# The inverse root of the row norms: from VectorE to GpSimd

## The chip, the cores and the metric

The kernel runs on one core of a Trainium2 chip as a single launch. The core has five engines with a queue each: TensorE (PE in the profile, with its weight loads apart as PEld), VectorE (DVE), ScalarE (ACT), GpSimd (POOL) and SyncE (SP, which here only issues DMAs). Each engine takes its instructions in a fixed order; an instruction that waits holds up everything behind it on its engine. The metric is the device time of one launch in microseconds (us), less is better.

## The reference

Two networks run one after the other on 256 tokens of width 1024. The first has two layers, each with a gated delta rule branch and a sliding window attention; the second has two layers, each of a gated feed-forward part, a mixer with two kinds of attention, and a second feed-forward part, on a latent stream and a context stream of 256 tokens each. What matters here is that every part ends by a norm over the 1024 columns of its output, a residual sum, and another norm over the sum that feeds the next part:

```python
def rmsnorm(x, g):
    xf = x.astype(jnp.float32)
    y = xf * lax.rsqrt(jnp.mean(xf * xf, axis=-1, keepdims=True) + EPS)
    return (y * g.astype(jnp.float32)).astype(x.dtype)
...
    mix = (jax.nn.sigmoid(gate_a) * y_a + jax.nn.sigmoid(gate_b) * y_b) @ w_o
    x = x + rmsnorm(mix, post_mix_g)

    h2 = rmsnorm(x, pre_mlp_g)
    ff = jnp.square(jax.nn.relu(h2 @ w_ff1)) @ w_ff2
    return x + rmsnorm(ff, post_mlp_g)
```

## The kernel before

All matrix products are made from weights that stream in from memory: `wtile` (L239) loads a raw tile by DMA, ScalarE makes its high part `hi` (L210) and VectorE the rest `lo` (L198), and TensorE adds three products for each tile (`mm3`, L264 to L266). Between these, VectorE also accumulates a product with the conditioning vector (`acc<-araw,csil,acc`, L201), which is needed later and has low priority.

A stream has 256 tokens, worked as two blocks of 128 (`tb` 0 and 1). `out_proj` (L1067) ends a part. For each block it makes two PSUM tiles of 512 columns. ScalarE squares both and sums the rows (`junk<-mm`, into the two columns of `ss`), and VectorE multiplies by the gain (`d`, or `acc` where partial sums were kept). Then, at a raised priority (`high_priority`, L1092), `inv_root` (L413) turns the two sums into 1/sqrt of their sum: `ms` is the sum, `rs` the integer guess, `rq_h` minus half of `ms`, and three Newton steps write `rq_t` and `rs` in turn. That is nine VectorE instructions on a single column of 128 rows, eight of them in a chain. The result scales `d` into the residual stream `xh` (or `xc`, the context; L201, two halves). At once the next norm of the same block begins (`nx.run`): `row_rs` (L420) squares the two halves of the new `xh` on ScalarE, calls `inv_root` again, and the row is scaled by the second root (`xn`, half by VectorE at L205, half by ScalarE at L210). The transposes of `xn` (TensorE, L405 in the first network and L1148 in the second) start the next part.

So each block of each part needs two inverse roots one behind the other, from the last product of the part to the first transposes of the next. The transposes are put off by `DEFER`: TensorE has products of the other block, and of the next weights, in between. A scheduler of the program's build sets the order of each engine's instructions, by priority and by when it takes an operand to be ready; a change of one engine's instructions can so reorder the others.

GpSimd makes four constants at the start and clears the tile `qz` twelve times (L1289) for the attentions of the second network; it has nothing else to do. The build calls `inv_root` 58 times: twice at the start, 28 times in `out_proj`, and for 28 rows that feed a next part. The other use of `rsqrt` (several columns at a time) isn't touched.

Of the kernel before, what the change touches and what calls it, by code (L numbers as in the profile page):

```python
# [11 lines left out]
I32 = mybir.dt.int32  # L12
AF = mybir.ActivationFunctionType
ALU = mybir.AluOpType
# [3 lines left out]
P = 128  # L18
# [16 lines left out]
MAGIC = 1597463007.0  # L35
# [128 lines left out]
class Kern:  # L164
# [38 lines left out]
    def ts(self, out, a, s1, op0, s2=None, op1=None):  # L203
        if op1 is None:
            self.nc.vector.tensor_scalar(out, a, s1, None, op0=op0)  # L205
        else:
            self.nc.vector.tensor_scalar(out, a, s1, s2, op0=op0, op1=op1)
# [203 lines left out]
        self.act(junk[:, :a.shape[-1]], a, AF.Square, scale=scale, accum_out=out)  # L411

    def inv_root(self, ss, eps):  # L413
        v = self.t(self.small, [P, 1], "ms", bufs=4)
        self.ts(v, ss[:, 0:1], ss[:, 1:2], ALU.add, eps, ALU.add)
        rs = self.t(self.small, [P, 1], "rs", bufs=4)
        self.rsqrt(rs, v, 1)
        return rs

    def row_rs(self, st, tb):  # L420

# [1086 lines left out]
```

## Time and profile before

| what | value |
|---|---|
| median of 3 runs (lowest, highest) | 2869.26 us (2864.54, 2869.78) |
| the profiled execution's own time | 2872.72 us |
| its span in the profile | 2870.9 us |
| granted clock of TensorE over the span | 0.989 |
| TensorE busy | 2790.4 us, 97% |
| VectorE busy | 2130.9 us, 74% |
| ScalarE busy | 1334.1 us, 46% |
| GpSimd busy | 5.2 us in 16 instructions |

The span runs from the first to the last instruction that the profile shows; 1.8 us of the profiled time lie outside it. Busy shares are means over the whole span, and TensorE's ends of instructions are modelled. Where TensorE waits is read from its idle time and from what ended it.

### The profile page before, as it was taken

How to read it: one execution, taken by the hardware profiler on the slowest of the kernel's cores; microseconds unless marked ns; L12 is line 12 of the kernel's file. 1: busy time of each engine (PE TensorE's matmuls, PEld its weight loads, DVE VectorE, ACT ScalarE, POOL GpSimd, SP SyncE). 2: the span in 40 equal slices, each digit the busy share in tenths (PEclk: the TensorE clock that was granted, in tenths of full speed). 3: DMA queues.
4: the chain of work that ended last, by engine and by line, in shares of the span. 5: the costliest groups of instructions: out<-in, count | busy, mean ns of one | idle time of the engine just before them, and what ended most of it. 6: DMA issues, size and time to landing. Idle time of an engine off the chain costs nothing.

```text
span 2870.9 us, 51232 instructions
## 1 busy us (share of the span) xinstructions
PE 2790.4 (97%) x19840; PEld 2594.7 (90%) x19840; DVE 2130.9 (74%) x5043; ACT 1334.1 (46%) x2627; POOL 5.2 (0%) x16
## 2 busy tenths in 40 slices
PE   8999999999999999999999999999999999999998
PEld 7999988889999888999988988998989989888897
DVE  7888668898886788878699788877686554766664
ACT  6555454565554655332243656332353323546553
POOL 0000000000000000000000000000000000000000
PEclk9999999999999999999999999999999999999999
DMA  6542457655325576455435242555444543341564
GB/s 220 171 118 72 142 178 236 201 181 159 92 74 177 175 222 198 136 159 160 134 114 167 77 138 82 165 151 162 138 131 141 150 125 96 98 131 44 153 197 140
DMA packets 443908, 416.76 MB, mean 145 GB/s; under 512 B 18320, under 2 KB 383760, under 8 KB 443664
## 3 DMA queue, kind: packets, MB, share of 16 engines
q1 hardware_dynamic: 443664, 413.49, 47.4%
q8 instruction: 156, 2.56, 0.4%
q14 instruction: 88, 0.72, 0.1%
HBM read 412.37 MB, written 1.05 MB: 144 GB/s over the span
## 4 chain that ended last, share of the span: by engine, by line
PE 81%; DVE 10%; ACT 4%; DMA 4%; issue 2%; SPq 0%; DVEq 0%; ACTq 0%
PE mm L264 22%; PE mm L265 22%; PE mm L266 22%; DVE lo L198 2%; PE sm L563 2%; PE sm L515 2%; ACT hi L210 2%; DMA araw<-in_w_ada 1%; PE sm L552 1%; PE sm L805 1%; DVE acc L201 1%; PE sm L800 1%; PE sm L264 1%; PE sm L265 1%; PE sm L266 1%
## 5 line engine op out<-in xcount | busy, mean ns | idle before, releaser
L198 DVE TENSOR_TENSOR lo<-raw,hi 128x1024 fp32r<-128x1024 f32 (+2 forms) x628 | 750.9, 1207 | 323.2 <-ACT hi L210 321.8
L210 ACT ACTIVATE hi<-raw 128x1024 fp32r<-128x1024 f32 (+2 forms) x628 | 647.9, 1047 | 717.4 <-PE mm L265 295.7
L264 PE MATMUL mm<-xTh,hi 128*128 128x256 f32 x2336 | 650.9, 279 | 3.0 <-ACT xTh L210 3.0
L265 PE MATMUL mm<-xTh,hi 128*128 128x256 f32 x2336 | 651.5, 279 | 0.8 <-DVE xTh L201 0.8
L266 PE MATMUL mm<-xTh,lo 128*128 128x256 f32 x2336 | 650.4, 279 | 0.0
L264 PEld LDWEIGHTS mm<-xTh,hi 128*128 128x128 f32 x2336 | 440.7, 189 | 3.7 <-ACT xTh L210 3.5
L265 PEld LDWEIGHTS mm<-xTh,hi 128*128 128x128 f32 x2336 | 441.3, 189 | 1.5 <-DVE xTh L201 1.2
L266 PEld LDWEIGHTS mm<-xTh,lo 128*128 128x128 f32 x2336 | 441.0, 189 | 0.1
L201 DVE SCALAR_TENSOR_TENSOR acc<-araw,csil,acc 128x256 f32<-128x256 f32 x896 | 391.3, 480 | 64.4 <-DMA araw<-in_w_ada 61.7
L264 PE MATMUL mm<-hi,hid 128*128 128x512 f32 x872 | 341.2, 391 | 0.0
L266 PE MATMUL mm<-hi,hid 128*128 128x512 f32 x872 | 340.3, 390 | 0.0
L265 PE MATMUL mm<-lo,hid 128*128 128x512 f32 x872 | 340.2, 390 | 0.0
L264 PE MATMUL mm<-xTc,hi 128*128 128x256 f32 x1104 | 306.2, 277 | 0.0
L265 PE MATMUL mm<-xTc,hi 128*128 128x256 f32 x1104 | 305.9, 277 | 0.0
L266 PE MATMUL mm<-xTc,lo 128*128 128x256 f32 x1104 | 305.6, 277 | 0.0
L265 PEld LDWEIGHTS mm<-xTc,hi 128*128 128x128 f32 x1104 | 207.3, 188 | 0.4
L264 PEld LDWEIGHTS mm<-xTc,hi 128*128 128x128 f32 x1104 | 207.3, 188 | 0.4
L266 PEld LDWEIGHTS mm<-xTc,lo 128*128 128x128 f32 x1104 | 207.3, 188 | 0.1
L266 PEld LDWEIGHTS mm<-hi,hid 128*128 128x128 f32 x872 | 164.0, 188 | 34.3
L265 PEld LDWEIGHTS mm<-lo,hid 128*128 128x128 f32 x872 | 164.2, 188 | 33.7 <-DVE lo L198 0.3
L264 PEld LDWEIGHTS mm<-hi,hid 128*128 128x128 f32 x872 | 164.1, 188 | 33.2
L264 PE MATMUL mm<-hi,xTh 128*128 128x256 f32 (+3 forms) x512 | 180.1, 353 | 4.9 <-ACT xTh L1157 3.4
(323 smaller groups left out, 4665.0 us busy)
## 6 DMA issues: line engine op xcount, KB each, us to landing
raw<-in_ffn_wi SPq DMA_DIRECT2D x352, 256.0 KB, 3.6
araw<-in_w_ada SPq DMA_DIRECT2D x288, 256.0 KB, 2.9
raw<-in_w_ff SPq DMA_DIRECT2D x128, 512.0 KB, 4.2
raw<-in_w_in SPq DMA_DIRECT2D x116, 512.0 KB, 3.9
raw<-in_ffn_wo SPq DMA_DIRECT2D x88, 512.0 KB, 4.1
raw<-in_w_o SPq DMA_DIRECT2D x40, 512.0 KB, 3.4
raw<-in_w_in SPq DMA_DIRECT2D x24, 432.0 KB, 4.8
raw<-in_w_up_sw SPq DMA_DIRECT2D x16, 512.0 KB, 3.8
```

The source lines that it names most:

```text
L198: self.nc.vector.tensor_tensor(out=out, in0=a, in1=b, op=op)
L201: self.nc.vector.scalar_tensor_tensor(out=out, in0=a, scalar=s, in1=b, op0=op0, op1=op1)
L210: self.nc.scalar.activation(out, a, func, **kw)
L264: mm(ps, lhsT=ah, rhs=bh, start=first, stop=False)
L265: mm(ps, lhsT=ah, rhs=bl, start=False, stop=False)
L266: mm(ps, lhsT=al, rhs=bh, start=False, stop=last)
L515: nc.tensor.matmul(ps[:, h, o:o + n], lhsT=q, rhs=k, start=m == 0, stop=m == len(qk) - 1)
L552: nc.tensor.transpose(ps[:, b, :], sc[:, b // nb, (b % nb) * P:(b % nb + 1) * P], self.ident)
L563: nc.tensor.matmul(po[:, h, :], lhsT=pT[:, h * nb + kb, :], rhs=v, start=kb == 0, stop=kb == nb - 1)
L800: nc.tensor.matmul(ps[:, i, :], lhsT=LT[:, i, :], rhs=Dm[:, i, :], start=True, stop=True)
L805: nc.tensor.matmul(ps[:, i, :], lhsT=DT[:, i, :], rhs=M[:, i, :], start=True, stop=True)
```

## The change

`inv_root` no longer calls `rsqrt`. It issues the same nine steps as GpSimd instructions on the same kind of columns; `t*(-0.5 v)` and `(t+1.5)*y` become one two-operation instruction each, with columns as scalars.

```diff
     def inv_root(self, ss, eps):
-        v = self.t(self.small, [P, 1], "ms", bufs=4)
-        self.ts(v, ss[:, 0:1], ss[:, 1:2], ALU.add, eps, ALU.add)
-        rs = self.t(self.small, [P, 1], "rs", bufs=4)
-        self.rsqrt(rs, v, 1)
-        return rs
+        v, y, nh, t = (self.t(self.small, [P, 1], x, bufs=4) for x in ("ms", "rs", "rq_h1", "rq_t1"))
+        ts = self.nc.gpsimd.tensor_scalar
+        ts(v, ss[:, 0:1], ss[:, 1:2], eps, op0=ALU.add, op1=ALU.add)
+        ts(y.bitcast(I32), v.bitcast(I32), -0.5, MAGIC, op0=ALU.mult, op1=ALU.add)
+        ts(nh, v, -0.5, None, op0=ALU.mult)
+        for _ in range(3):
+            ts(t, y, y, nh, op0=ALU.mult, op1=ALU.mult)
+            ts(y, t, 1.5, y, op0=ALU.add, op1=ALU.mult)
+        return y
```

The build also gives other orders. At the start of GpSimd's queue stood the constants, and behind them the first clearing of `qz`. Now there stand, behind the constants, an instruction without operands (its line is that of the first step) and the nine steps of the first root (`ms_103` from the sums `ss_98`; `rs_104` is the root):

```order
L1508 UNCONDITIONAL_BRANCH
L416 ISA
L416 TENSOR_SCALAR ms_103<-ss_98 128x1
L417 TENSOR_SCALAR rs_104<-ms_103 128x1
L418 TENSOR_SCALAR rq_h_16_105<-ms_103 128x1
L420 TENSOR_SCALAR rq_t_17_106<-rs_104,rq_h_16_105 128x1
L421 TENSOR_SCALAR rs_104<-rq_t_17_106,rs_104 128x1
L420 TENSOR_SCALAR rq_t_17_106<-rs_104,rq_h_16_105 128x1
L421 TENSOR_SCALAR rs_104<-rq_t_17_106,rs_104 128x1
L420 TENSOR_SCALAR rq_t_17_106<-rs_104,rq_h_16_105 128x1
L421 TENSOR_SCALAR rs_104<-rq_t_17_106,rs_104 128x1
```

All 58 roots stand there in this form, 522 instructions; the clearings of `qz` come between them.

On VectorE, at the end of the first layer's mixer (block 0, the row `xn_4356` of `xh_78`), this stood before between the multiplication by the gain `gpre` and the scaling by the second root `rs_4364`:

```order
L198 TENSOR_TENSOR xn_4356<-xh_78,gpre_364 128x1024
L207 TENSOR_SCALAR ms_4362<-ss_4357 128x1
L198 TENSOR_TENSOR lo_4497<-raw_4502,hi_4496 128x1024
L207 TENSOR_SCALAR rs_4364<-ms_4362 128x1
L205 TENSOR_SCALAR rq_h_738_4366<-ms_4362 128x1
L198 TENSOR_TENSOR d_4406<-mm_4379,gbc_4238 128x512
L201 SCALAR_TENSOR_TENSOR rq_t_737_4365<-rs_4364,rq_h_738_4366 128x1
L198 TENSOR_TENSOR lo_4507<-raw_4508,hi_4506 128x1024
L201 SCALAR_TENSOR_TENSOR rs_4364<-rq_t_737_4365,rs_4364 128x1
L198 TENSOR_TENSOR lo_4517<-raw_4518,hi_4516 128x1024
...
L205 TENSOR_SCALAR xn_4356<-xn_4356,rs_4364 128x512
```

The same place after the change, from the same multiplication on (the root is now `rs_4363`):

```order
L198 TENSOR_TENSOR xn_4356<-xh_78,gpre_364 128x1024
L198 TENSOR_TENSOR lo_4497<-raw_4498,hi_4496 128x1024
L205 TENSOR_SCALAR xn_4356<-xn_4356,rs_4363 128x512
L198 TENSOR_TENSOR lo_4497<-raw_4502,hi_4496 128x1024
L198 TENSOR_TENSOR d_4406<-mm_4379,gbc_4238 128x512
L198 TENSOR_TENSOR lo_4507<-raw_4508,hi_4506 128x1024
L198 TENSOR_TENSOR lo_4517<-raw_4518,hi_4516 128x1024
```

The scaling moved ahead of three weight splits and one multiplication by the gain; it stands behind one split only, and holds up those behind it until GpSimd's root is there.

On TensorE, at the end of a feed-forward part of the second network (context block 0, `xn_16747`), the transposes stood before behind eight products of the tile `mm_16910`, which belongs to a later block:

```order
L266 MATMUL mm_16810<-hi_2535_16644,hid_16523 128x512
L264 MATMUL mm_16910<-hi_16614,hid_15587 128x512
L265 MATMUL mm_16910<-lo_16615,hid_15587 128x512
...
L265 MATMUL mm_16910<-lo_16615,hid_15880 128x512
L1148 MATMUL sm_16839<-cst_76,xn_16747 128x128 x4
L1148 MATMUL sm_16851<-cst_76,xn_16747 128x128 x4
```

Now they stand in front of them (L1152 is the same line of the changed file):

```order
L266 MATMUL mm_16810<-hi_2535_16644,hid_16523 128x512
L1152 MATMUL sm_16839<-cst_76,xn_16747 128x128 x4
L1152 MATMUL sm_16851<-cst_76,xn_16747 128x128 x4
L264 MATMUL mm_16910<-hi_16614,hid_15587 128x512
L265 MATMUL mm_16910<-lo_16615,hid_15587 128x512
```

The transposes moved ahead of eight products. The transposes stand ahead of work that they stood behind at eleven more of the 26 places where a block's norm lies between two parts, by one to some fifty products each; at most of the others they stand where they stood.

## Rows read from the trace of the kernel before

**Rows 1.** The page's first part: busy us, share of the span, instructions.
```profile
PE 2790.4 (97%) x19840; PEld 2594.7 (90%) x19840; DVE 2130.9 (74%) x5043; ACT 1334.1 (46%) x2627; POOL 5.2 (0%) x16
```

**Rows 2.** Waits of PE by what ended them: us in total, times, longest us.
```profile
PE sm L405 <- DVE xn L205: 20.8, 5, 10.7
...
PE sm L1148 <- DVE xn L205: 8.7, 6, 2.5
```

**Rows 3.** Timeline of DVE, then PE, first layer's mixer end: start us, us, what [idle].
```profile
368.62 0.21 DVE L207 TENSOR_SCALAR ms<-ss 128x1 f32<-128x1 f32 x1 [4.50 <-ACT junk L210]
...
370.74 0.16 DVE L201 SCALAR_TENSOR_TENSOR rs<-rq_t,rs 128x1 f32<-128x1 f32 x1
...
374.54 0.21 DVE L207 TENSOR_SCALAR ms<-ss 128x1 f32<-128x1 f32 x1
374.67 1.22 DVE L198 TENSOR_TENSOR lo<-raw,hi 128x1024 fp32r<-128x1024 f32 x1
...
380.19 0.16 DVE L201 SCALAR_TENSOR_TENSOR rs<-rq_t,rs 128x1 f32<-128x1 f32 x1
...
378.07 0.39 PE L265 MATMUL mm<-lo,mT 128*128 128x512 f32 x1
378.29 0.39 PE L266 MATMUL mm<-hi,mT 128*128 128x512 f32 x1
380.93 1.18 PE L405 MATMUL sm<-cst,xn 128*128 128x128 f32 x8 [2.25 <-DVE xn L205]
```

**Rows 4.** Timeline of DVE, then PE, at context block 0 of the second network.
```profile
1472.44 0.21 DVE L207 TENSOR_SCALAR ms<-ss 128x1 f32<-128x1 f32 x1
...
1475.92 0.16 DVE L201 SCALAR_TENSOR_TENSOR rs<-rq_t,rs 128x1 f32<-128x1 f32 x1
...
1478.47 0.21 DVE L207 TENSOR_SCALAR ms<-ss 128x1 f32<-128x1 f32 x1
...
1482.34 0.15 DVE L201 SCALAR_TENSOR_TENSOR rs<-rq_t,rs 128x1 f32<-128x1 f32 x1
...
1483.64 1.07 PE L1148 MATMUL sm<-cst,xn 128*128 128x128 f32 x8 [2.52 <-DVE xn L205]
```

**Rows 5.** Stretches behind two such waits: busy (count) PE, PEld, DVE, ACT, POOL, clock.
```profile
382.00:385.50 3.50, 3.34 (x16) 3.23 (x16) 3.40 (x10) 0.74 (x2) 0.00 (x0) 0.51 0.69 209
385.50:389.00 3.50, 3.50 (x31) 3.50 (x31) 3.41 (x7) 2.98 (x7) 0.00 (x0) 1.00 0.73 253
...
586.90:590.30 3.40, 2.82 (x9) 2.08 (x8) 3.40 (x9) 0.00 (x0) 0.00 (x0) 0.50 0.26 92
590.30:593.70 3.40, 3.40 (x11) 3.14 (x10) 1.17 (x6) 1.18 (x2) 0.00 (x0) 0.50 0.54 153
593.70:597.00 3.30, 3.30 (x18) 3.15 (x17) 2.77 (x6) 2.08 (x4) 0.00 (x0) 1.00 0.40 94
```

**Rows 6.** Timeline of PE: the three other transposes that waited over 2.2 us.
```profile
569.50 1.67 PE L405 MATMUL sm<-cst,xn 128*128 128x128 f32 x8 [2.97 <-DVE xn L205]
...
585.13 1.07 PE L405 MATMUL sm<-cst,xn 128*128 128x128 f32 x8 [2.52 <-DVE xn L205]
...
944.24 1.16 PE L405 MATMUL sm<-cst,xn 128*128 128x128 f32 x8 [2.28 <-DVE xn L205]
```

**Rows 7.** Instructions on the tiles rs and ms: ns min/median/max, first to last.
```profile
L207 DVE TENSOR_SCALAR ms<-ss x58: 162/210/216, 7.5 to 2863.7; 128x1 f32<-128x1 f32 x58
L207 DVE TENSOR_SCALAR rs<-ms x58: 142/148/155, 7.8 to 2864.4; 128x1 int32<-128x1 int32 x58
L205 DVE TENSOR_SCALAR rq_h<-ms x58: 141/145/150, 7.8 to 2864.4; 128x1 f32<-128x1 f32 x58
...
L201 DVE SCALAR_TENSOR_TENSOR rq_t<-rs,rq_h x174: 177/217/223, 8.0 to 2865.5; 128x1 f32<-128x1 f32 x174
L201 DVE SCALAR_TENSOR_TENSOR rs<-rq_t,rs x174: 122/158/163, 8.3 to 2865.8; 128x1 f32<-128x1 f32 x174
```

**Rows 8.** Timeline of DVE: first and last of the 58 roots.
```profile
7.51 0.21 DVE L207 TENSOR_SCALAR ms<-ss 128x1 f32<-128x1 f32 x1
...
9.16 0.16 DVE L201 SCALAR_TENSOR_TENSOR rs<-rq_t,rs 128x1 f32<-128x1 f32 x1
...
2863.65 0.21 DVE L207 TENSOR_SCALAR ms<-ss 128x1 f32<-128x1 f32 x1 [4.75 <-ACT junk L210]
...
2865.77 0.16 DVE L201 SCALAR_TENSOR_TENSOR rs<-rq_t,rs 128x1 f32<-128x1 f32 x1
```

**Rows 9.** Timeline of POOL.
```profile
0.34 0.11 POOL L1500 MEMSET const-uint8-127<- 128x1 uint8 x1
1505.68 2.75 POOL L1289 MEMSET qz<- 64x384 f32 x6 [1505.23 <-PE mm L266]
```

## The prediction

> **What bounds the kernel now.** I read the busy times first. TensorE is busy for 2790.4 us, 97% of a span of 2870.9 us, and GpSimd for 5.2 us [rows 1]. So the 1.6 us or so of VectorE work per root are worth nothing as work: only places where TensorE stands still can be won or lost. I therefore read the waits of TensorE next, by what ended them. Two rows belong to this change: transposes of a normed row `xn` that wait for VectorE's scaling of it, 20.8 us in 5 waits in the first network and 8.7 us in 6 in the second [rows 2]. One of the eleven, of 10.7 us, is the start of the kernel. The other ten make 20.8 + 8.7 - 10.7 = 18.8 us; five of them are longer than 2.2 us.
>
> Third, the two timelines around such a wait. At the end of the first layer's mixer the first root runs from 368.62 to 370.90, the second from 374.54 to 380.35, with a 1.22 us weight split `lo` in the middle of it; TensorE's other products end at 378.68, and the transposes start at 380.93 after 2.25 us of idleness [rows 3]. The two chains are 2.28 + 5.81 = 8.09 us. At context block 0 of the second network they are 3.64 + 4.02 = 7.66 us, and the wait is 2.52 us [rows 4].
>
> Fourth, the stretch behind a wait. For 3.5 us after the transposes of that first place the granted clock is 0.51, the lower level (1.2 GHz), and TensorE gets through 16 products; in the next 3.5 us the clock is 1.00 and it does 31 [rows 5]. That wait so costs another 1.7 us. The five waits over 2.2 us are this one, that of context block 0 and three more of 2.97, 2.52 and 2.28 us [rows 6]. I read such a stretch behind each, and behind the one at 585 us it is twice as long, 586.9 to 593.7 at a clock of 0.50 [rows 5]: six times 1.7 = 10.2 us. In all, what a better or worse root can move at these places is 18.8 + 10.2 = 29 us, 1% of the time, and a good deal more if it gets worse.
>
> **The change, part by part.** *Nine instructions leave VectorE, 58 times.* By the medians one root is 0.210 + 0.148 + 0.145 + 3 x (0.217 + 0.158) = 1.63 us of busy time [rows 7], 94 us in all, out of an engine that is busy for 74% [rows 1]. From start to end a chain with nothing between its steps takes 1.81 us (7.51 to 9.32), one with one multiplication between 2.28 us (2863.65 to 2865.93) [rows 8]; with splits between, 3.6 to 5.8 us [rows 3, 4]. What leaves is therefore not 1.8 us of a path but often twice that, because other work of VectorE sits inside the chain.
>
> *Nine instructions come to GpSimd.* Nothing can sit inside them there but a clearing of `qz`. No row shows a GpSimd instruction that reads anything. Two rows bound one step. A clearing of one column takes 0.11 us, and six clearings of 64x384 take 2.75 us, 0.46 each [rows 9]. VectorE's step is 1.81 / 9 = 0.20. A dependent step has to read, compute and write one column: more than the first row, with far fewer elements than the second. I take 0.30, the middle, above VectorE's own step; this is an estimate. With 0.2 us for the hand-over from ScalarE and to VectorE (an estimate, about one VectorE step) a root takes L = 9 x 0.30 + 0.2 = 2.9 us. Its ends are 9 x 0.11 + 0.2 = 1.2 and 9 x 0.46 + 0.2 = 4.3 us.
>
> *What this does at a place.* New wait = old wait + 2L - old pair + the work that the transposes were moved ahead of. At the mixer's end nothing moved: 2.25 + 5.80 - 8.09 is below 0, the wait is gone, and the slow stretch with it. At context block 0 the transposes now stand ahead of eight products of 0.22 us from start to start (378.07 to 378.29 in [rows 3]), 1.8 us: 2.52 + 5.80 - 7.66 + 1.8 = 2.5, no gain at all. I made the same sum at all 26 places, with the spare time of those that do not wait now. The waits add up to 0.5 us for L = 1.8, 1.3 for 2.0, 5.6 for 2.5, 11.2 for 2.9, 13 for 3.0, 27 for 3.5, 46 for 4.0 and 58 for 4.3; waits over 2 us are none up to 2.5, two at 2.9, five at 3.5, about fifteen at 4.3. The sum is steep, because the order has spent the slack: where transposes moved forward, nothing covers a longer root.
>
> *The ends.* At the start and the end nothing covers a root. The first goes from 1.81 to 2.9 (+1.1), the last from 2.28 to 2.9 (+0.6), and the second block of the start is late by about as much as the first (+1): +2.7 us.
>
> *VectorE's order.* The scaling by the root now stands behind one `lo` and in front of three and a `d`, and holds them up until GpSimd is done. VectorE is busy for 3.40 of 3.50 us just there [rows 5], so this cover is not free: per block it no longer does 2 x 1.63 = 3.3 us of steps, and stands at the scaling for up to 2.9 us less a `lo` of 1.22 at each root, 2 x 1.7 = 3.4 us. The two cancel: 0.
>
> *The clearings and the instruction without operands.* A clearing stands at worst between the two roots of a block, where GpSimd has nothing to do from 370.90 to 374.54 [rows 3], 3.6 us against the 2.75 of six clearings: 0. The instruction without operands runs once. Its length is in no row; it can start at about 0.45, after the constants, and the first root is wanted at 7.51 [rows 9, 8], so 7 us of it are hidden and each further one costs 1 us: I take 0. The Trainium skill ("GPSIMD Engine Reference", 2.1 Instruction dispatch) gives about 6 us for the first call to freshly loaded code, which no row here shows and which would just be hidden.
>
> *Sum.* Waits 11.2 - 18.8 = -7.6; slow stretches 2 x 1.7 - 10.2 = -6.8; ends +2.7; together -11.7 us. The profiled execution took 2872.72 us (span and 1.8 around it), so 2861.0; it lies 3.5 us above the median of the runs, 2869.26, from which the sum gives 2857.5. At L = 2.0: -17.5 - 10.2 + 0.5 = -27, 2842. At L = 4.3: +38.7 waits, +15 slow stretches, +7 ends = +61, 2930. The turn lies at about L = 3.25.
>
> **The rivals.** *VectorE and GpSimd hold each other off (slower).* While a root runs, VectorE runs a `lo` of 1.22 us with two operands in memory [rows 3]. If GpSimd's first step waits for the end of it, half of 1.22 on the mean goes on top: L = 3.5. Then waits of 27, +8.2; five waits over 2 us as before, so 0 for the slow stretches; ends +4.5: +13, 2882. It decides from a hold of 0.35 us per root (2.9 to 3.25). For it: VectorE is nearly always busy where roots run [rows 5]. Against: it holds only a first step, since VectorE soon stands still at the scaling. Chance 0.20. The Trainium skill ("SBUF — State Buffer", Who interferes with whom) states it as a rule: a VectorE instruction with two inputs in SBUF and a GpSimd instruction that reads SBUF exclude each other, and the second one blocks. GpSimd read nothing in the run before, so no row agrees or disagrees; by that rule the sum is this rival's.
>
> *A step is as long as the upper row (slower).* 0.40 gives L = 3.8: waits of 38, four or five more slow stretches, ends +5.4, about +33, 2902; 0.46 gives 2930. For it: of the rows of GpSimd only the one with data is a clearing of 0.46 [rows 9]. Against: that clears 384 columns. Chance 0.18. The Trainium skill ("GPSIMD Engine Reference", 3 Performance versus the Vector engine) calls VectorE roughly twice as fast for elementwise work; twice the 0.20 of [rows 8] would be the 2902 of this rival.
>
> *It comes to nothing.* A root of about 3.25 us, or splits that VectorE does later behind its scaling so that TensorE waits for `lo` where it waited for `xn`: 2869, give or take 5. For it: the 3.3 against 3.4 us above, and that moved transposes eat the gain wherever the order changed, as at context block 0. Against: VectorE has 26% of idle time in which to catch up [rows 1]. Chance 0.20.
>
> **How the numbers follow.** The forecast, L from 2.0 to 3.0, has 0.42; its own range is 2842 to 2863, and the time 2857.5. A measurement of this kernel tells about 0.2%, 5.7 us, from no change. Faster than that are the forecast and a little of the third rival: 0.43. Slower are the first two, less a little of the first: 0.37. The same: 0.20. The range begins at 2842, the forecast's lower end, and goes through the third and first rivals to 2905, just over the milder size of the second; beyond it lies a step of over 0.4, and below it one of less than 0.2, together under 2 in 10.
>
> **What would show it.** GpSimd's rows on `ms`, `rs` and the two others, 522 instructions: the start-to-start time of two steps is the 0.30, and a first step that starts only when a `lo` ends is the first rival. The wait at the mixer's end should be gone, with a granted clock of 1.00 behind it, and that at context block 0 still be near 2.5. Transposes' waits for `xn` should make about 11 us besides the start, which should be 1 to 2 us later. VectorE should have about 94 us less. I am wrong if the step is over 0.34 us, if other waits of TensorE (for `lo`, or in the attentions, whose order also moved) grow by more than 10 us, or if the start is held by the instruction without operands.

## The result, and the profile after

The changed kernel takes 2973.4 us in the median (2968.28 to 2980.3, 4 runs), against 2866.9 for the kernel before (2863.92 to 2869.78, 4 runs): a ratio of 1.0364, 95% interval 1.0344 to 1.0384. It is 106.5 us slower. The forecast was 2857.5 in a range from 2842 to 2905.

The first part of the page, for [rows 1]:

```profile
PE 2820.3 (95%) x19840; PEld 2618.9 (88%) x19840; DVE 2070.9 (70%) x4521; ACT 1330.7 (45%) x2627; POOL 179.2 (6%) x538
```

The span is 2978.5 us, 107.6 longer. TensorE's busy time grew by 29.9 us with the same 19840 products, while the granted clock fell from 0.989 to 0.973; the other 77.7 us are idleness. The idleness by what ended it, for [rows 2] (L1152 is L1148 of before, L1161 is L1157, L1129 is L1125):

```profile
PE sm L1152 <- DVE xn L205: 39.3, 14, 6.8
PE mm L264 <- ACT xTh L210: 18.5, 8, 5.9
PE sm L405 <- DVE xn L205: 14.5, 4, 11.5
PE mm L264 <- ACT xTh L1161: 13.3, 3, 9.5
PE mm L266 <- DVE xTh L198: 12.6, 4, 4.4
...
PE sm L1129 <- ACT w L210: 5.8, 2, 4.9
PE sm L1129 <- DVE w L207: 5.7, 1, 5.7
PE sm L1129 <- ACT gate L1130: 4.7, 1, 4.7
```

For `xTh` and the gates the kernel before had these rows:

```profile
PE mm L264 <- ACT xTh L210: 4.2, 7, 1.5
PE mm L264 <- ACT xTh L1157: 3.4, 2, 1.8
...
PE sm L1125 <- ACT w L210: 1.0, 2, 0.7
...
PE mm L266 <- DVE xTh L198: 0.6, 1, 0.6
```

The transposes now wait 39.3 + 14.5 - 11.5 (the start) = 42.3 us for a normed row, 18.8 before. That is the part the prediction had a sum for. The other rows hardly existed before: products that wait for `xTh`, the copies of those transposes (18.5 + 13.3 + 12.6 = 44 us; the same three rows made 8.2), and transposes in the second network that wait for the gates (L1129, 16.2 us against 1.0). The three groups grew by 23.5, 36 and 15 us; with the 29.9 us of TensorE's busy time that is nearly all of the 107.6.

The steps themselves, for [rows 7] (ns min/median/max; the last line is the idleness of VectorE and ScalarE that GpSimd's root ended, us and times):

```profile
L416 POOL TENSOR_SCALAR ms<-ss x58: 293/634/2412, 5.9 to 2969.8; 128x1 f32<-128x1 f32 x58
L417 POOL TENSOR_SCALAR rs<-ms x58: 190/191/1251, 6.2 to 2970.2; 128x1 int32<-128x1 int32 x58
L418 POOL TENSOR_SCALAR rq_h<-ms x58: 218/218/1096, 6.5 to 2970.5; 128x1 f32<-128x1 f32 x58
...
L420 POOL TENSOR_SCALAR rq_t<-rs,rq_h x174: 334/340/1234, 7.7 to 2972.4; 128x1 f32<-128x1 f32 x174
L421 POOL TENSOR_SCALAR rs<-rq_t,rs x174: 264/265/267, 8.1 to 2972.8; 128x1 f32<-128x1 f32 x174
...
  POOL rs L421: 241.4, 85
```

Medians and minima agree except in the first step, whose shortest is 293 ns and whose median is 634: something holds it. VectorE and ScalarE together stand 241.4 us for a root, 157 of it VectorE's.

The nine steps are longer than VectorE's, but the whole root isn't: from the start of `ms` to the end of the last step it takes 3.77 us in the mean of the 58, from 3.28 to 5.41; on VectorE, counted the same way in the kernel before, it took about 3.8, from 1.80 to 9.74, since other work of VectorE ran between its steps.

The same place as in [rows 3], the first layer's mixer end, now on GpSimd, VectorE, ScalarE and TensorE:

```profile
372.08 0.29 POOL L416 TENSOR_SCALAR ms<-ss 128x1 f32<-128x1 f32 x1 [354.22 <-ACT junk L210]
...
375.10 0.27 POOL L421 TENSOR_SCALAR rs<-rq_t,rs 128x1 f32<-128x1 f32 x1
378.63 0.75 POOL L416 TENSOR_SCALAR ms<-ss 128x1 f32<-128x1 f32 x1 [3.26 <-ACT junk L210]
...
382.11 0.27 POOL L421 TENSOR_SCALAR rs<-rq_t,rs 128x1 f32<-128x1 f32 x1
...
378.00 1.22 DVE L198 TENSOR_TENSOR lo<-raw,hi 128x1024 fp32r<-128x1024 f32 x1
382.41 0.49 DVE L205 TENSOR_SCALAR xn<-xn,rs 128x512 f32<-128x512 f32 x1 [3.19 <-POOL rs L421]
382.81 1.22 DVE L198 TENSOR_TENSOR lo<-raw,hi 128x1024 fp32r<-128x1024 f32 x1
...
393.18 1.42 DVE L201 SCALAR_TENSOR_TENSOR xh<-d,rs,xh 128x512 f32<-128x512 f32 x2 [2.59 <-POOL rs L421]
394.51 0.69 DVE L198 TENSOR_TENSOR xTh<-sm,xTh 128x512 fp32r<-128x512 f32 x1
...
382.41 0.72 ACT L210 ACTIVATE xn<-xn,rs 128x512 f32<-128x512 f32 x1 [2.92 <-POOL rs L421]
...
383.61 1.99 ACT L210 ACTIVATE hi<-raw 128x1024 fp32r<-128x1024 f32 x2
387.68 1.06 ACT L210 ACTIVATE hi<-raw 128x1024 fp32r<-128x1024 f32 x1 [2.08 <-DMA raw<-in_w_ff]
...
389.21 1.07 ACT L210 ACTIVATE xTh<-sm 128x512 fp32r<-128x512 f32 x2
...
382.95 1.09 PE L405 MATMUL sm<-cst,xn 128*128 128x128 f32 x8 [0.88 <-DVE xn L205]
389.85 0.58 PE L264 MATMUL mm<-hi,xTh 128*128 128x256 f32 x1 [5.80 <-ACT xTh L210]
...
395.25 0.58 PE L266 MATMUL mm<-hi,xTh 128*128 128x256 f32 x1 [3.76 <-DVE xTh L198]
```

Read it from the bottom. The transposes themselves wait less than before, 0.88 us for 2.25: the two roots take 3.29 (372.08 to 375.37) and 3.75 us, 7.04 for 8.09. But then TensorE stands for 5.80 and 3.76 us. The transposes are done at 384.04, and ScalarE copies them at 389.21: first come three parts `hi` of the next weights, one of which waits 2.08 us for its load, and two squares of the other block. VectorE's half of the copy stands at 394.51 behind the other block's `xh`, which waits 2.59 us for that block's root. 0.88 + 5.80 + 3.76 = 10.4 us at a place that cost 2.25. ScalarE's rows there in the kernel before had the copies right behind the row:

```profile
379.73 1.06 ACT L210 ACTIVATE hi<-raw 128x1024 fp32r<-128x1024 f32 x1 [0.26 <-DMA raw<-in_w_ff]
380.69 0.71 ACT L210 ACTIVATE xn<-xn,rs 128x512 f32<-128x512 f32 x1
381.62 1.12 ACT L210 ACTIVATE xTh<-sm 128x512 fp32r<-128x512 f32 x2 [0.22 <-PE sm L405]
```

The clock behind it, for [rows 5]:

```profile
384.10:389.80 5.70, 0.00 (x0) 0.00 (x0) 3.93 (x4) 3.62 (x7) 0.39 (x1) 0.65 0.69 195
389.90:393.40 3.50, 1.60 (x6) 1.30 (x6) 0.91 (x3) 0.38 (x1) 2.47 (x9) 0.50 0.90 274
...
396.00:399.50 3.50, 3.50 (x19) 3.50 (x18) 2.06 (x3) 0.31 (x2) 2.52 (x6) 0.50 0.52 185
```

The granted clock falls during the first wait (0.65 in the mean of that stretch) and stays at the lower level (1.2 GHz) until past the second; at full clock 31 products fit where 19 are here.

### The profile page after: what moved, and what is told of

Read it like the earlier page. It is cut to its first block, busy times and chain, and to the rows that moved or that the text cites. A ratio compares the mean times of both kernels' runs of the same rounds, so it can differ in the third digit from the quotient of the medians.

```text
span 2978.5 us, 51363 instructions
## 1 busy us (share of the span) xinstructions
PE 2820.3 (95%) x19840; PEld 2618.9 (88%) x19840; DVE 2070.9 (70%) x4521; ACT 1330.7 (45%) x2627; POOL 179.2 (6%) x538
## 4 chain that ended last, share of the span: by engine, by line
issue 64%; PE 23%; POOL 6%; DVE 4%; ACT 1%; DMA 1%; POOLq 0%; DVEq 0%; SPq 0%; ACTq 0%
PE mm L265 6%; PE mm L266 6%; PE mm L264 6%; POOL rq_t L420 2%; POOL rs L421 2%; POOL ms L416 1%; DVE acc L201 1%; PE sm L567 1%; DVE lo L198 1%; PE sm L519 1%; PE sm L809 1%; PE sm L804 1%; DMA araw<-in_w_ada 1%; PE sm L556 1%; POOL rq_h L418 1%
## 5 line engine op out<-in xcount | busy, mean ns | idle before, releaser
L416 POOL TENSOR_SCALAR ms<-ss 128x1 f32<-128x1 f32 x58 | 38.3, 660 | 2653.9 <-ACT junk L210 2219.9
```

What stands on the lines that cost most here:

```text
L416: ts(v, ss[:, 0:1], ss[:, 1:2], eps, op0=ALU.add, op1=ALU.add)
```

## The experiments

The times of e1 to e15 are single runs, each beside a run of the kernel before on the same chip, which took 2867.2 us for e1 to e4, 2877.3 for e5 to e8, 2864.8 for e9 to e12 and 2865.6 for e13 to e15. Differences are to that run; single runs of the kernel before scatter by some 8 us to either side, so differences under 10 us say little.

**e1, one Newton step on GpSimd.**

```diff
-        for _ in range(3):
+        for _ in range(1):
             ts(t, y, y, nh, op0=ALU.mult, op1=ALU.mult)
```

> GpSimd's root with one Newton step in place of three (the root is less exact; nothing else is left out). In the changed kernel two steps take 0.81 us (0.34 + 0.10 + 0.26 + 0.10), so a root alone should take 3.29 - 1.62 = 1.67 us. Theory, held engines (the time is lost because VectorE and ScalarE stand in line at a scaling that waits for GpSimd, so that what is behind it, the splits and the copies of the transposes, comes late): the holds shrink by 1.6 us each, and most of the loss goes: 2860 to 2890 us, TensorE's waits for xTh under 15 us. Rival, the order (the build's new order costs by itself, whatever the root's length): at least two thirds of the loss stays, over 2935 us. Rival, length alone (a root is what a block waits for, nothing else): 2842 to 2860 by the sum of the prediction at L = 2.0 to 2.4.

2896.35 us, +29. A root takes 2.10 us in the mean, shorter than VectorE's before in most places, and the waits for `xn` fall to 11.7 us, below the kernel before. The waits for `xTh` are still 28.6 us. So 77 of the 106 us come with the length of GpSimd's root, which is also the time that VectorE and ScalarE stand for it (124 us in all, from 241), and a loss stays where length cannot be the reason. The measured time lies just above the span given for held engines, whose other sign, waits for `xTh` under 15 us, did not come; it is no support for length alone.

**e2 and e3, one kind of root on GpSimd, the other on VectorE.** e2: the 30 roots of the norms that feed a part; e3: the 28 that end a part. (`inv_root_dve` is the old function.)

```diff
-                rs = self.inv_root(ss, eps)
+                rs = self.inv_root_dve(ss, eps)
```

> Only the roots of the norms that feed a next part (30 of 58) run on GpSimd; those that end a part stay on VectorE. Held engines: the second root's scaling is shared by VectorE and ScalarE, so both stand, and what waits behind them is the next part's own operands; more than half of the loss of 107 us: 2925 to 2950 us. Length alone: half the roots, half the loss, 2905 to 2925.

> Only the 28 roots that end a part run on GpSimd. Held engines: only VectorE stands at these (the scaling of d into xh), ScalarE has no scaling of its own by this root; less than half of the loss: 2885 to 2915 us. Length alone: 2905 to 2925, as with the other half. If the two halves together come to much less than 107 us, the two holds of a block add up beyond what each costs.

2915.24 (+48) and 2922.29 (+55). Together 103 of 106 us: the two kinds cost the same within the scatter, and add up. The held-engines forecast, that the second root costs more since two engines stand at it, was wrong; both times lie in the spans given for length alone.

**e4, a long root on VectorE.** Seven Newton steps.

> All roots on VectorE as in the kernel before, with seven Newton steps in place of three: by the steps of the kernel before (0.45 us for two in a chain without other work) a root takes 1.81 + 4 x 0.45 = 3.6 us, as long as GpSimd's, and VectorE has 87 us more work. Other work of VectorE can run between its steps, and VectorE stands for nobody. Held engines: TensorE's waits for xn grow, those for xTh don't; +10 to +45 us, 2880 to 2915. Length alone: as the changed kernel or worse, 2960 to 3000.

2930.09, +63: between the two spans. The expectation counted a root without other work between its steps, 3.6 us; in the run it takes about 6.9 us in the mean, from 3.65. So a root nearly twice as long as GpSimd's costs VectorE's kernel three fifths of what GpSimd's costs, with 57 us of added busy time on VectorE in it. TensorE's waits of both kinds:

```profile
PE sm L405 <- DVE xn L205: 30.0, 3, 15.6
PE sm L1148 <- DVE rq_t L201: 12.1, 4, 7.0
...
PE sm L405 <- DVE rs L201: 11.2, 1, 11.2
PE sm L1148 <- DVE xn L205: 8.1, 7, 2.7
PE mm L264 <- ACT xTh L1157: 7.2, 5, 1.8
...
PE mm L264 <- ACT xTh L210: 3.3, 3, 1.5
```

The transposes (L405 and L1148, whichever VectorE instruction the profile names) wait about 46 us besides the start (15.6), somewhat more than in the changed kernel (42.3), but the products wait 10.5 us for `xTh` and not 44. A late row alone thus does not make the loss of 106 us: the late copies came only with the roots on GpSimd.

**e5 and e6, transposes and copies raised.** All of a row's transposes and their copies are issued at the root's priority, in the changed kernel (e5) and in the kernel before (e6).

```diff
+        def first():
+            with self.k.tc.high_priority(offset=300):
+                back()
-        self.k.deferred.append([DEFER * 800, (st.name, tb), back])
+        self.k.deferred.append([DEFER * 800, (st.name, tb), first])
```

> The changed kernel, and the transposes of a normed row with the copies of them (xTh) are issued at the priority of the root: on ScalarE the two copies at the mixer's end then stand behind one square and one split, where in the changed kernel they stand behind two squares and three splits, and before the change right behind the row. Theory, queues (a good part of the loss is that the copies stand behind work which is itself late): TensorE's waits for xTh, 44 us in the changed kernel, fall to 10 to 25; with the clock some 25 to 45 us less, 2930 to 2950 us. Rival, the held engines alone (what is behind a held scaling is late in any order): xTh waits over 35, time over 2960.

> The same raised priority in the kernel before, where the copies already stand right behind the row. Queues and held engines alike: no change, 2860 to 2872 us.

e5: 3028.57 (+151), against both theories; e6: 2879.39 (+2), as expected. In e5 the waits for `xTh` are gone (under 5 us), but the transposes moved forward on TensorE too and stand there for the row: waits for `xn` of 126 us. The edit moved two things; it only shows that the copies' lateness is a matter of order, and that an earlier place for the transposes is worth nothing while the root is late.

**e7, GpSimd's steps by themselves.** Chains of roots beside one kind of work at a time.

> A program of its own that computes none of the reference: chains of GpSimd roots in nine stretches, alone, beside VectorE instructions of several kinds, beside ScalarE, and three of these VectorE instructions without GpSimd. In the changed kernel a root alone takes 3.29 us and the mean one 3.77. Theory, exclusion: beside 128x1024 differences of two tiles in SBUF each GpSimd step can wait for the end of one, 1.2 us, so a root goes to 6 to 12 us; beside products with one operand in PSUM it stays at 3.3; beside ScalarE too. VectorE's own instructions get longer by less than 0.3 us each. Rival, hand-over: the 0.3 to 0.9 us on the first step come from the wait for ScalarE's sum and not from VectorE; then a root takes 3.3 us in every stretch. No theory is sure of the products with one operand in SBUF: 3.3 to 6 us.

The timeline beside VectorE's differences of two tiles in SBUF, and the same differences without GpSimd:

```profile
17.39 15.18 DVE L1476 TENSOR_TENSOR lo<-a,b 128x1024 f32<-128x1024 f32 x12
...
17.54 1.13 POOL L1466 TENSOR_SCALAR ms<-ms 128x1 f32<-128x1 f32 x1
18.75 1.18 POOL L1467 TENSOR_SCALAR rs<-ms 128x1 int32<-128x1 int32 x1
19.99 1.21 POOL L1468 TENSOR_SCALAR rq_h<-ms 128x1 f32<-128x1 f32 x1
21.31 1.30 POOL L1470 TENSOR_SCALAR rq_t<-rs,rq_h 128x1 f32<-128x1 f32 x1
...
97.96 15.09 DVE L1476 TENSOR_TENSOR lo<-a,b 128x1024 f32<-128x1024 f32 x12
```

One GpSimd step goes through for each VectorE instruction: 1.26 us a step, where steps of 0.19 to 0.34 us stand alone. A whole root would take 9 x 1.26 = 11.3 us. VectorE pays nothing: 15.18 us for 12 instructions, 15.09 without GpSimd. In the other stretches a root of a chain (its first step runs beside the root ahead of it) takes in the mean 3.0 us beside products with one operand in PSUM, 3.0 beside ScalarE, 3.1 alone (one step there is held by a lone addition of two SBUF tiles), and 4.1 beside single-operand products in SBUF of 0.43 us each; beside `scalar_tensor_tensor` with two operands in SBUF (128x512) a step takes about 0.8 us. Exclusion holds; the rival (a hand-over) falls. The Trainium skill ("SBUF — State Buffer", Who interferes with whom) states that a VectorE instruction with two inputs in SBUF contends with a GpSimd instruction that reads SBUF, and this trace agrees: with one of the two in PSUM the hold is gone.

**e8, two Newton steps on VectorE** in the kernel before (`range(2)`).

> The kernel before with two Newton steps in place of three on VectorE (the root is less exact by some parts in a million). A root alone is shorter by 0.45 us, interleaved ones by up to 1 us. By the sum of the prediction, 26 places with 2 x 0.45 us less each: waits for xn from 18.8 to about 13, one or two of the six slow stretches less: 2857 to 2865 us. Rival, order (any change of VectorE's instructions rearranges the queues, and that weighs more than the length): 2850 to 2890, with waits elsewhere that grow by as much.

2857.72 beside 2877.34, -20; waits for `xn` fell from 18.8 to 8.0 us. The time is inside its span. The root is a little less exact. Timed below as e16.

**e9 to e11, the row scaled by one engine alone.**

```diff
-            self.ts(xn[:, :512], xn[:, :512], rs, ALU.mult)
-            self.act(xn[:, 512:], xn[:, 512:], scale=rs)
+            self.act(xn, xn, scale=rs)
```

(and the same for the second network; e10 has `self.ts` alone.)

> The changed kernel with the row xn scaled by the second root on ScalarE alone (both halves), so that VectorE stands only at the first root of a block. Held engines: VectorE's idle time until a GpSimd root, 157 us in the changed kernel, falls to 75 to 90, the splits behind it come in time, and TensorE loses 15 to 40 us less than in the changed kernel: 2935 to 2960 us. Length alone: the scaling is on the path and gets longer (0.72 to about 1.05 us), 2975 to 2995.

> The changed kernel with the row scaled on VectorE alone, so that ScalarE never stands at a GpSimd root (85 us of idleness in the changed kernel). Held engines: the parts hi and the copies xTh come in time, 10 to 35 us less than the changed kernel, 2940 to 2965. Length alone: 2970 to 2990, since the scaling gets longer by some 0.4 us.

> The control for the row on ScalarE, with the roots on VectorE as before: the longer scaling by itself, 30 times 0.3 us at most, 2865 to 2885 us in both theories.

e9: 2987.16 (+122); e10: 2973.93 (+109); the control e11: 2870.30 (+6). Neither gave anything back: both times lie in the spans given for length alone, and the plain form of the held-engines theory fell. In e9 VectorE did stand for less (76 us instead of 157), but a root's mean length rose from 3.77 to 4.18 us: with VectorE free to go on with its splits, GpSimd is held off more (79 of its steps are lengthened, 46 in the changed kernel). In e10 ScalarE no longer stands for the root, and then waits for loads instead: at the mixer's end 4.02 us for a raw tile, and TensorE waits for the copies as long as in the changed kernel (5.83 us, there 5.80). The waits for `xTh` stay at 37 and 39 us.

**e12, no raised priority.** `HP = 0` in the changed kernel.

> The changed kernel without the raised priority of the root and of what follows it (offset 0 in place of 300). Theory, queues: the scalings stand later in the queues of VectorE and ScalarE, behind more work, so these two are held for less, 90 to 130 us instead of 157 on VectorE; but the row comes later, so the waits for xn grow. 2950 to 2990 us. Rival, length alone: only the second of the two happens, over 2990.

2945.49, +81, a little better than its span and no support for length alone. VectorE stands for 143 us, hardly less; what fell is the wait for VectorE's half of the copies (12.6 to 2.6 us), since the other block's `xh` no longer goes before it.

**e13 to e15, the places in the queues put back.** Four edges of order: a row's scaling behind the other block's last square (ScalarE) and last multiplication by the gain (VectorE), and the other block's `xh` and squares behind the copies of the first. The scaling is also issued later, shortly before the transposes, and so no longer at the raised priority.

```diff
+    def behind(self, ins):
+        return self.tc.issue_after(getattr(ins, "ins", ins)) if ins is not None else ExitStack()
...
+                with self.behind(self.last_d):
+                    self.ts(xn[:, :512], xn[:, :512], rs, ALU.mult)
+                with self.behind(self.last_sq):
+                    self.act(xn[:, 512:], xn[:, 512:], scale=rs)
...
+            with self.behind(self.last_hi):
+                self.square_sum(st.x[:, tb, i * 512:(i + 1) * 512], ss[:, i:i + 1], 1.0 / 32)
...
+                    with self.behind(self.last_lo):
+                        self.stt(x, ds[c], rs, x, ALU.mult, ALU.add)
```

ScalarE's order at the mixer's end shows what that does. Changed kernel:

```
L210 ACTIVATE xn_4356<-xn_4356,rs_4363 128x512
L210 ACTIVATE junk_4404,ss_4378<-mm_4379 128x512
L210 ACTIVATE hi_4506<-raw_4508 128x1024
L210 ACTIVATE hi_4516<-raw_4518 128x1024
L210 ACTIVATE hi_4516<-raw_4522 128x1024
L210 ACTIVATE junk_4433,ss_4378<-mm_4408 128x512
L210 ACTIVATE xTh_4354<-sm_4437 128x4x128
L210 ACTIVATE xTh_4354<-sm_4444 128x4x128
```

e13 (the kernel before has the same order, but for the numbers and for the square, which there stands one place earlier, ahead of the last `hi`):

```
L212 ACTIVATE hi_4514<-raw_4520 128x1024
L212 ACTIVATE junk_4431,ss_4376<-mm_4406 128x512
L212 ACTIVATE xn_4356<-xn_4356,rs_4363 128x512
L212 ACTIVATE xTh_4354<-sm_4437 128x4x128
L212 ACTIVATE xTh_4354<-sm_4444 128x4x128
```

> The changed kernel with four places in the queues fixed: the scaling of a row by the second root stands behind the other block's last square on ScalarE and its last multiplication by the gain on VectorE, and the other block's xh and its squares stand behind the copies xTh of the first. ScalarE's order at the mixer's end is then that of the kernel before. Theory, order: waits for xTh fall from 44 us to 8 to 20, VectorE is idle at GpSimd's roots for 60 to 110 us instead of 157; what stays is the longer root: 2900 to 2935 us. Rival, the stand itself: VectorE works on while a root runs, GpSimd is held off more, a root gets as long as 4.5 us in the mean, and the time stays over 2950.

> The same four places with one Newton step (the root is less exact). Order: the 29 us that one step still lost go, 2850 to 2875 us. Rival: 2885 us or more.

> The control: the same four places fixed in the kernel before, where most of them are as they would be anyway. 2860 to 2880 us in either theory.

e13: 2926.00 (+60), inside the span for order; e14: 2880.42 (+15), between its two spans; the control e15: 2876.92 (+11), inside its span. Waits of TensorE, and engines standing for a root, in e13:

```profile
PE sm L1167 <- DVE xn L207: 33.9, 12, 6.9
PE sm L407 <- DVE xn L207: 31.4, 4, 11.5
...
PE mm L266 <- ACT xTh L212: 4.0, 6, 1.5
...
PE mm L268 <- DVE xTh L200: 2.0, 3, 1.1
...
  POOL rs L423: 129.4, 47
```

The order accounts for 46 us of the 106 as measured, 57 if what the edges cost VectorE's kernel (11) is taken off, each to within some 10 us. The waits for `xTh` are at 8 us with a third row of 1.8, as before the change, and VectorE and ScalarE stand for 129 us instead of 241. The rival was right in one thing: VectorE works on while a root runs, the mean root grows from 3.77 to 4.54 us, and the waits for `xn` from 42 to 33.9 + 31.4 - 11.5 = 54 us. With one step (e14) what is left over the control is 4 us, within the scatter. The two accounts overlap: less the control, the order is worth 57 us with three steps and about 25 with one (29 - 4), so the 77 us of e1 and these 57 can't be added. The order costs more when the engines stand longer.

**e16, two steps on VectorE, timed.**

> The kernel before with two Newton steps on VectorE, timed against it. One look gave 2857.7 beside 2877.3 us. If the shorter root is what counts (waits for xn 18.8 to 8.2 us there, and two of the slow stretches less), a ratio of 0.992 to 0.997, clear of no change; if that look was the chip's scatter, 0.997 to 1.003.

2861.83 us (12 runs) against 2869.11 (17 runs): a ratio of 0.9972, interval 0.9962 to 0.9982: clear of no change, and just short of the gain in the span given. It is the one version that beats both kernels, and it keeps the root where it was.

## Why the prediction was wrong

**Right.** TensorE bounds the kernel and the loss shows as its idleness and clock. The sum over the places held: it gives about 44 us of waits for `xn` at an L of 3.97 us (the measured 3.77 and the hand-over, estimated at 0.2; at the mixer's end it was 0.13), and 42.3 were measured. By place: the mixer's end, 2.25 + 7.04 - 8.09 = 1.2 (measured 0.88); context block 0 of the second network, with roots of 3.80 and 3.66 us, 2.52 + 7.46 - 7.66 + 1.8 = 4.1 (measured 3.67). The clearings, the instruction without operands (the first root starts at 5.86 us, at once with its sums) and the ends (+2.7 forecast; the first wait grew by 0.7, the last root by 1.0) were about as sized. One sum is off without effect: at L = 4.3 the waits grow by 58 - 18.8 = 39.2, not 38.7.

**Mis-sized: the length.** A step was taken as 0.30 us. Alone it takes 0.19 to 0.34 and about 0.1 to the next, 3.29 / 9 = 0.37 in the mean, so a root is 3.29 us. Then comes the rival that had 0.20: GpSimd is held off by VectorE. 42 of the 58 roots have a step that is lengthened, 36 times the first, until a VectorE instruction ends (of 46 lengthened steps 19 end with a `lo`, 12 with the multiplication by the gain, on `acc`); the mean over all roots is 0.49 us. The rival put 0.6 us on a root of 2.9; it was 0.5 on one of 3.3. With the hand-over, L is 3.97 where the forecast had 2.9: on the mean no shorter than VectorE's root, so nothing was gained there, and the waits for `xn` went up by 23.5 us where they should have fallen by 7.6. The prediction had named a step over 0.34 us, and other waits that grow by more than 10 us, as signs of being wrong; both came.

**The step that failed: "VectorE's order", put at 0**, because work given up and time stood cancel in VectorE's busy time. They do not by amount: VectorE's busy time fell by 60 us and not by 94 (steps had overlapped a neighbour, as in [rows 3], where a `lo` starts at 374.67 while `ms` runs to 374.75), and VectorE stands 157 us at the roots, 2.8 us each time and not 1.7. And the place counts. A scaling early in the queue stops everything behind it, and the copies of the transposes, which the build had put behind splits and squares, come late. At the mixer's end a load is late too: the `lo` behind the scaling ends at 384.03, the next weights are issued at 384.06, and ScalarE's `hi` waits for them until 387.68; over the whole kernel ScalarE's waits for raw tiles did not grow (99 us, 101 before). The prediction read the orders of VectorE and TensorE and no row of ScalarE's, where the copies had moved from right behind the row to behind three splits and two squares. In place of the 0, products waited 36 us more for `xTh` and transposes 15 us more for the gates. e13 puts the order at 46 to 57 us with its share of the clock.

**The clock.** The forecast gave back 6.8 us; TensorE's products took 29.9 us more. Seventeen waits besides the start are now over 3 us; behind those at the mixer's end the clock is at the lower level, as it was behind the longest ones before.

**Open.** How far standing and order can be told apart: e9, e10 and e13 each removed some of the standing, e13 changed the order with it, and the exclusion grew when VectorE stood less (e9, e13). A form of the splits without two operands in SBUF was not tried, so the length without exclusion is known only from e7.

## What to carry to other kernels

A chain of tiny steps costs its length on the engine that runs it, and on every engine whose queue has a consumer of it: look at what stands behind that consumer on each, ScalarE and the loads too, before the order's cost is put at nothing. On an idle engine a step can be slower than on the busy one (here 0.37 us against 0.20), and the engines that need the result stand for the whole chain where before other work ran inside it. Equal length from start to end is then no equal cost: about 3.8 us a root on either engine, 106 us apart. Shortening the chain where it was (one Newton step less) gained 0.28%; moving it lost 3.6%.

## What the runs showed of the hardware

Beside VectorE instructions with two operands in SBUF, GpSimd's single-column steps pass one for one, 1.26 us a step with 128x1024 operands, while VectorE loses under 1% (15.18 against 15.09 us); with one operand in PSUM GpSimd runs at its own 3.0 us a root. Where VectorE stood less for GpSimd, more of GpSimd's steps were held and the roots grew longer: 46 steps and 3.77 us a root in the changed kernel, 79 and 4.18 in e9, 111 and 4.54 in e13.
